# A two-layer streaming encoder in split fp32: sums of x, the last pair's factors and weight-sum transfers moved in the MLP

## The chip, the core and the metric

The kernel runs on one core of a Trainium2 chip. The metric is the device time of one execution in microseconds (us). The core has five engines that run side by side and meet only at semaphores: PE (TensorE, matrix products), DVE (VectorE), ACT (ScalarE), POOL (GpSimd) and SP (SyncE), of which SP and POOL here mostly start transfers. Each engine works off its own instructions in the order in which they were written out for it.

## The reference

Input is a prompt of 512 frames and a sample of 64 frames, model width 1024, so 576 columns of x in all. Layer 0 mixes tokens by pooling, layer 1 by sparse attention with a learned choice of keys. Each is followed by the same MLP, which takes most of the time and is what the change touches:

```python
def _mlp(h, w_up, w_down):          # w_up 1024 x 4096, w_down 4096 x 1024
    u = jax.nn.relu(h @ w_up)
    return (u * u) @ w_down

for i in range(DEPTH):              # 2 layers
    h = _rmsnorm(x, norm_mix[i])
    x = x + mixer(i, h)             # pooling mixer, or attention
    x = x + _mlp(_rmsnorm(x, norm_mlp[i]), mlp_w_up[i], mlp_w_down[i])
y = _rmsnorm(x, norm_final)
```

All of it is float32, and besides y the new pooling states and keys and values are returned.

## The kernel before

**Split products.** A float32 number is held as a high part (rounded by a cast) and a low part (the rest). A product of weights w and activations u is made of three matmuls: wh by uh, wh by ul, wl by uh. Each matmul has a 128x128 piece of weights and 288 columns, half of the 576 (HT).

**Units of weights.** Weights come in as raw blocks of 128x512 (256 KB) by transfers that SP starts. `split_unit` makes a unit of one: ACT casts the high part (wh, line 181), DVE subtracts it for the low part (wl, line 182). Six units can be held at a time. `made` yields units in the order in which they are used, and `next_unit(ahead=4)` draws from it until five are in hand and gives the first.

**Seven products for eight.** In the MLP the weight blocks are taken in pairs ("even" and "odd"), and two by two blocks of weights and of activations are multiplied with seven products in place of eight. This needs sums of weight blocks and seven factors of the activations (t3, t1, t2, b11, b22, b21, t4, numbered 0 to 6 in the tiles v and u). One sum of weights, s1, is loaded by a transfer of SP and one of POOL that adds to it in flight; a third transfer adds the even block to the odd one in place (`pair_sums`, lines 236 to 238); two further sums are made by DVE (lines 260 and 264). s1 and the second sum come from a pool of 3 buffers. `seven` makes one task of it: seven products of 12 matmuls each, in PSUM banks b, a and c; after a bank is complete a step of `Up` or `Down` reads it.

**A layer's MLP.** The hidden 4096 rows go in four chunks. Chunk 0's up projection is plain: eight blocks `up` (line 305), each pair giving one u (lines 455 to 483). While these run, DVE and ACT also make the factors of x that the later chunks need: `x_sums(j)` for j = 0 to 3 (tiles rough and xt, lines 431 to 435; one xt tile each; called after blocks 2, 3, 4 and 5), and `x_difference` after block 7 (tiles snap and xs, lines 440 to 443). Then chunk 0's down projection runs, four tasks `Down(q)`, each adding into x (line 536). Chunks 1 to 3 have four `Up(c, j)` tasks and then four `Down` tasks (three in the last chunk of layer 1). An `Up` task reads its banks (lines 565, 579, 585), squares on ACT (line 455), makes the seven factors in v (lines 476 to 483) and splits them into u by `parts_of`: a cast on ACT (line 472) and a subtraction on DVE (line 473). The tile v has one buffer, u has four, one for each pair of the chunk. The first product of a `Down` task is b11 over all four pairs, so it ends with the last pair's b11; the steps lo0, hi1, hi0 and lo1 of `Up` stand behind its last four products (b21, t3, b22, t4), in that order.

**What sets the order.** Nothing is ordered by hand on an engine. A scheduler takes the instructions in the order in which the code issues them, with waiting and buffers, and may let those of one engine pass each other; so a move in the code changes rows on every engine, which the section on the change shows.

## Time and profile before

| | |
|---|---|
| median of 3 runs | 1117.95 us (1115.55 to 1118.61) |
| profiled execution | 1120.28 us, its span 1118.5 us |
| mean granted clock of PE | 0.984 |
| PE busy | 1063.2 us, 95% of the span |
| DVE busy | 913.1 us, 82% |
| ACT busy | 626.0 us, 56% |
| POOL busy | 263.2 us, 24% |
| read from memory | 141.15 MB |

Times in the views are us from the start of the span. A row of the timeline gives start, length, engine, line, operation, output and inputs, and in brackets the idle time of the engine before it with the instruction that ended it. A matmul's length in such a row overlaps with the next one's, so the distance of two starts tells more than a length.

### The profile page before, as it was taken

The numbers are of one execution on the slowest core, as the hardware profiler recorded it, in microseconds if no ns is written. First come the engines' busy times: TensorE is split into PE (matmuls) and PEld (weight loads), VectorE is DVE, ScalarE is ACT, GpSimd is POOL, SyncE is SP. The second block draws the span as 40 slices with busy tenths as digits, with TensorE's granted clock in tenths as the row PEclk, the third lists the DMA queues.
The fourth block names the chain that finished last, engine by engine and source line by source line (L and its number), as shares of the span: only waits on it lengthen the run. The fifth ranks groups of instructions, "written<-read, shape, count | busy, mean of one in ns | idle before, by whom it ended". The sixth has DMA issues, their size and how long they took to land.

```text
span 1118.5 us, 21674 instructions
## 1 busy us (share of the span) xinstructions
PE 1063.2 (95%) x7942; PEld 1030.8 (92%) x7942; DVE 913.1 (82%) x1831; ACT 626.0 (56%) x1226; POOL 263.2 (24%) x285
## 2 busy tenths in 40 slices
PE   8998999999899899999989999999999999899896
PEld 8998999999899888999978888998998999899895
DVE  7788889879878967779997944689889879879974
ACT  8555456447546636354377776455457447547641
POOL 3100111111111100218696893000111111111101
PEclk9998999999999999999998999998999999999998
DMA  8222767576577564456641444433667566576512
GB/s 247 89 76 76 170 159 161 146 175 153 141 173 166 143 175 129 123 170 157 204 124 48 147 145 135 138 78 77 171 163 168 143 166 163 142 165 166 126 54 86
DMA packets 94459, 157.66 MB, mean 141 GB/s; under 512 B 13729, under 2 KB 25296, under 8 KB 94352
## 3 DMA queue, kind: packets, MB, share of 16 engines
q1 hardware_dynamic: 68720, 109.80, 32.3%
q0 software_dynamic: 15840, 28.84, 16.4%
q10 hardware_dynamic: 9792, 17.63, 5.2%
q8 instruction: 62, 1.02, 0.4%
q14 instruction: 45, 0.37, 0.1%
HBM read 141.15 MB, written 10.89 MB: 136 GB/s over the span
## 4 chain that ended last, share of the span: by engine, by line
PE 74%; DVE 12%; issue 5%; DMA 4%; ACT 2%; POOL 1%; SPq 1%; ACTq 0%; DVEq 0%; POOLq 0%
PE b L496 27%; PE c L496 14%; PE up L305 8%; PE a L496 7%; PE pj L305 3%; PE wo L305 3%; DVE wl L182 2%; PE wa L305 2%; PE sc L1219 2%; PE pt L1245 1%; PE pb L953 1%; DVE u L473 1%; PE o L1277 1%; PE dn L305 1%; PE o L1270 1%
## 5 line engine op out<-in xcount | busy, mean ns | idle before, releaser
L181 ACT CAST wh<-raw 128x512 fp32r<-128x512 f32 (+1 forms) x316 | 194.7, 620 | 247.6 <-PE b L496 86.5
L182 DVE TENSOR_TENSOR wl<-raw,wh 128x512 fp32r<-128x512 f32 (+1 forms) x294 | 205.7, 703 | 32.3 <-ACT wh L181 28.0
L496 PE MATMUL b<-u,wh 128*128 128x288 f32 x992 | 206.1, 299 | 21.1 <-DVE u L473 9.2
L496 PEld LDWEIGHTS b<-u,wh 128*128 128x128 f32 x992 | 160.3, 189 | 26.9 <-DVE u L473 11.0
L181 ACT CAST wh<-sum 128x512 fp32r<-128x512 f32 x165 | 101.8, 620 | 93.0 <-PE b L496 46.1
L496 PE MATMUL b<-u,wl 128*128 128x288 f32 x496 | 146.3, 297 | 0.0
L182 DVE TENSOR_TENSOR wl<-sum,wh 128x512 fp32r<-128x512 f32 x165 | 113.0, 688 | 32.8 <-ACT wh L181 27.6
L496 PE MATMUL c<-u,wh 128*128 128x288 f32 x496 | 105.4, 300 | 0.2
L238 POOL DMA_DIRECT2D raw<-in_w_down x31 | 26.7, 863 | 321.3 <-DMA raw<-in_w_down 111.8
L496 PEld LDWEIGHTS b<-u,wl 128*128 128x128 f32 x496 | 93.7, 190 | 0.3 <-DVE wl L182 0.2
L305 PE MATMUL up<-xs,wh 128*128 128x288 f32 x512 | 91.7, 302 | 1.0 <-DVE v L463 1.0
L473 DVE TENSOR_TENSOR u<-v,u 128x576 fp32r<-128x576 f32 (+3 forms) x86 | 80.0, 932 | 9.0 <-ACT u L472 8.4
L496 PE MATMUL b<-xt,wh 128*128 128x288 f32 x384 | 78.7, 298 | 8.4 <-DVE v L579 8.4
L496 PEld LDWEIGHTS c<-u,wh 128*128 128x128 f32 x496 | 81.4, 191 | 2.1 <-DVE x L536 1.5
L305 PEld LDWEIGHTS up<-xs,wh 128*128 128x128 f32 x512 | 77.3, 194 | 1.9 <-DVE v L463 1.5
L472 ACT CAST u<-v 128x576 fp32r<-128x576 f32 (+3 forms) x86 | 69.6, 815 | 14.5 <-DVE v L480 8.4
L496 PE MATMUL b<-xs,wh 128*128 128x288 f32 x384 | 77.5, 295 | 0.0
L496 PE MATMUL c<-u,wl 128*128 128x288 f32 x248 | 74.1, 299 | 0.0
L496 PEld LDWEIGHTS b<-xt,wh 128*128 128x128 f32 x384 | 61.1, 188 | 11.2 <-DVE v L579 11.2
L305 PE MATMUL pj<-xs,wh 128*128 128x288 f32 x352 | 61.9, 295 | 1.3 <-ACT xs L294 1.3
L455 ACT ACTIVATE v<-v 128x288 f32<-128x288 f32 (+1 forms) x112 | 51.8, 475 | 17.1 <-DVE v L565 10.0
L496 PEld LDWEIGHTS b<-xs,wh 128*128 128x128 f32 x384 | 61.4, 188 | 0.0
(281 smaller groups left out, 2692.1 us busy)
## 6 DMA issues: line engine op xcount, KB each, us to landing
raw<-in_w_up SPq DMA_DIRECT2D x128, 256.0 KB, 3.0
raw<-in_w_down SPq DMA_DIRECT2D x128, 256.0 KB, 3.1
raw<-in_w_o ACTq DMA_DIRECT2D x32, 256.0 KB, 3.2
sum<-in_w_down SPq DMA_DIRECT2D x31, 256.0 KB, 3.1
sum<-in_w_down POOLq DMA_DIRECT2D x31, 256.0 KB, 4.7
raw<-in_w_down POOLq DMA_DIRECT2D x31, 256.0 KB, 4.5
raw<-in_w_in ACTq DMA_DIRECT2D x30, 256.0 KB, 3.2
sum<-in_w_up SPq DMA_DIRECT2D x24, 256.0 KB, 2.9
```

The lines of the kernel that those rows point to most:

```text
L181: act.copy(h, src)
L182: how["sub"].tensor_tensor(l, src, f32(h), ALU.subtract)
L238: pool.dma_start(raw, even[:, :512], accum_op=ALU.add)
L305: pe.matmul(pt[h][:, :m] if isinstance(pt, tuple) else pt[:, h, :m], wt, xs[k][:, part, c:c + m], start=(k == 0 and i == 0), stop=(k == n ...
L455: act.activation(v, v, AF.Square)
L472: act.copy(u[:, f, 0], v[:, f])
L473: dve.tensor_tensor(u[:, f, 1], v[:, f], f32(u[:, f, 0]), ALU.subtract)
L496: pe.matmul(bank[:, :HT], wt, ut, start=first and j == 0 and i == 0, stop=j == 3 and i == 2, skip_group_check=True)
L953: pe.matmul(pt[:, c0:c0 + rhs.shape[1]], lhs, rhs, start=n == 0, stop=n == len(steps) - 1)
L1219: pe.matmul(pt[:, hh, :nw], q[:, 2 * s + hh], ks[g][:, part, :nw], start=part == 0, stop=part == 1)
L1245: pe.transpose(pp[:, c:c + P], pr[:, hh, kt * P:(kt + 1) * P], ident)
L1270: pe.matmul(oc[:, 2 * s + hh], pT[:, c:c + P], V[:, kt, vs], start=kt == 0, stop=kt == i)
```

## The change

Four edits, all in the MLP; the computation stays the same.

1. The transfers for s1 go out with the pair's first block instead of with the odd block (`sum_of`); only the addition of the even block to the odd one stays there. The pool of sums has 4 buffers instead of 3.
2. In `seven`, units are drawn one at a time at fixed places (`ahead`, after each bank's step, up to LEAD = 5 in hand) instead of by `next_unit`.
3. In `Up`, the last pair of a chunk splits its factor 3 (b11) by itself right behind lo0 and factor 4 in hi0. In the other pairs factors 3 and 4 are split in hi0 instead of hi1. Factors 0 to 2 are split in lo1 instead of hi0.
4. `x_sums` 0 and 1 are issued after plain blocks 3 and 5, and 2 and 3 after the loop over the blocks, ahead of `x_difference`.

```diff
--- before.py
+++ after.py
@@ -49,6 +49,7 @@
 MLP_BLOCKS = ("up", "even", "odd", "down")
 PLAIN_CHUNKS = 1
 SEEDED = 4
+LEAD = 5
 UP_ORDER = (0, 4, 1, 5, 2, 6, 3, 7)
 FACTORS = ("t3", "t1", "t2", "b11", "b22", "b21", "t4")
 
@@ -211,10 +212,11 @@
                 raw.append(raw_tile(pool_, size)[:, :n // 2])
                 self.live[at].append(raw[-1])
                 (nc.sync if mlp else act).dma_start(raw[-1], src[:, i * n // 2:(i + 1) * n // 2])
+                if kind == "even" and i == 0:
+                    self.even, self.sum = src, sum_of(jobs[1][1])
                 if kind == "odd" and i == 0:
-                    self.blocks[-1][3].append(pair_sums(raw[0], self.even, src))
-                if kind == "even":
-                    self.even = src
+                    pool.dma_start(raw[0], self.even[:, :512], accum_op=ALU.add)
+                    self.blocks[-1][3].append(self.sum)
                 if i:
                     jobs.pop(0)
 
@@ -230,12 +232,11 @@
             self.fill()
             return self.blocks.pop(0) if self.blocks else None
 
-    def pair_sums(raw, even, odd):
+    def sum_of(odd):
 
         s1 = phase["sums"].tile([P, 512], F32, tag="sum", name=uid("sum"))
         nc.sync.dma_start(s1, odd[:, :512])
         pool.dma_start(s1, odd[:, 512:], accum_op=ALU.add)
-        pool.dma_start(raw, even[:, :512], accum_op=ALU.add)
         return s1
 
     def made():
@@ -498,32 +499,50 @@
 
         tasks = [0]
 
+        def ahead(n=1):
+
+            how["sub"] = dve
+            for _ in range(n):
+                if len(ready) < LEAD:
+                    u = next(units, None)
+                    if u is not None:
+                        ready.append(u)
+
+        def take():
+            if not ready:
+                ahead()
+            return ready.pop(0)
+
         def seven(operand, late, on):
 
 
             b, a_, c = (psum1(t) for t in "bac")
             on.banks = [t[:, :HT] for t in (a_, b, c)]
-            w = next_unit()
+            w = take()
             product(b, w, operand, "b11", rows, True)
             tasks[0] += 1
             if tasks[0] <= SEEDED:
                 pe.matmul(a_[:, :HT], w[0][:, :P], operand(0, "b11", 0), start=True, stop=True, skip_group_check=True)
             act.copy(a_[:, :HT], b[:, :HT])
-            w1 = next_unit()
+            ahead()
+            w1 = take()
             if late:
-                w2 = next_unit()
+                w2 = take()
                 product(c, w1, operand, "t1", rows[:3], True)
                 product(b, w2, operand, "t2", rows[:3])
                 product(c, w1, operand, "t1", rows[3:])
                 on.c()
+                ahead()
                 product(b, w2, operand, "t2", rows[3:])
             else:
                 product(c, w1, operand, "t1", rows, True)
                 on.c()
-                product(b, next_unit(), operand, "t2", rows)
+                ahead()
+                product(b, take(), operand, "t2", rows)
             on.b()
+            ahead()
             for bank, factor, then in ((a_, "b21", on.lo0), (b, "t3", on.hi1), (c, "b22", on.hi0), (b, "t4", on.lo1)):
-                product(bank, next_unit(), operand, factor, rows)
+                product(bank, take(), operand, factor, rows)
                 then()
 
         class Down:
@@ -543,21 +562,25 @@
 
             def lo0(self):
                 self.update(self.lo[0], 0, ALU.add)
+                ahead()
 
             def hi1(self):
                 self.update(self.hi[1], 1, ALU.subtract)
+                ahead()
 
             def hi0(self):
                 self.update(self.hi[0], 2, ALU.add)
+                ahead()
 
             def lo1(self):
                 self.update(self.lo[1], 1, ALU.subtract)
+                ahead()
 
         class Up:
 
 
             def __init__(self, c, j):
-                self.at = c, j
+                self.at, self.final = (c, j), j == half - 1
                 self.v, self.u = tiles()
 
             def relu(self, i, src, op, h):
@@ -573,12 +596,15 @@
 
             def lo0(self):
                 self.relu(3, self.banks[0], ALU.max, 1)
+                ahead()
+                if self.final:
+                    parts_of(self.u, self.v, slice(3, 4))
 
             def hi1(self):
                 v = self.v
                 dve.tensor_tensor(v[:, 4], self.banks[1], snap[:, 0], ALU.add)
                 self.relu(4, v[:, 4], ALU.min, 0)
-                parts_of(self.u, v, slice(3, 5))
+                ahead()
 
             def hi0(self):
                 v = self.v
@@ -586,15 +612,22 @@
                 self.relu(0, v[:, 0], ALU.max, 0)
                 if end and self.at[0] == 3:
                     left_over(self.at[1], v[:, 0])
+                parts_of(self.u, v, slice(4 if self.final else 3, 5))
                 first_sum(v)
                 middle_sums(v)
-                parts_of(self.u, v, slice(0, 3))
 
             def lo1(self):
                 v = self.v
                 self.relu(5, self.banks[1], ALU.min, 1)
+                if not self.final:
+                    ahead()
+                parts_of(self.u, v, slice(0, 3))
                 last_sum(v)
+                if not self.final:
+                    ahead()
                 parts_of(self.u, v, slice(5, 7))
+                if self.final:
+                    ahead(2)
 
         def spread():
 
@@ -646,8 +679,11 @@
                     for t in todo:
                         finished(*t)
                     todo.clear()
-                    if c == 0 and 2 <= i < 6:
-                        x_sums(i - 2)
+                    if c == 0 and 3 <= i < 7 and i % 2:
+                        x_sums(i // 2 - 1)
+                if c == 0:
+                    x_sums(2)
+                    x_sums(3)
                 if c == PLAIN_CHUNKS - 1:
                     snap = halves(tmp("snap", "s2", 1))
                     for j in range(half):
@@ -1415,13 +1451,13 @@
     with stage(more=RAWS[1]):
         with stage(xs=1, slots=1, tmps=6, ps=3, po=2):
             pool_mixer()
-        with stage(xs=1, u=1, acts=1, xt=1, sums=3, ps=2, po=4):
+        with stage(xs=1, u=1, acts=1, xt=1, sums=4, ps=2, po=4):
             mlp(0, 1, late=KT)
     with stage(under=1, xs=1, slots=1, cst2=1, tmps=5), ExitStack() as parts:
         const([P, UNDER], "pad", pool=phase["under"])
         parts.enter_context(stage(ps=2, po=4))
         attention(parts)
-    with stage(u=1, xs=1, acts=1, xt=1, sums=3, more=RAWS[1], ps=2, po=4):
+    with stage(u=1, xs=1, acts=1, xt=1, sums=4, more=RAWS[1], ps=2, po=4):
         mlp(1, 3, end=last)
```

On the engines this gives DVE and ACT six instructions more each, and the same number of transfers. Three places in the order:

The passage from an up phase to its down phase, on DVE. Here v_2317 is the last pair of chunk 1 in layer 0, u_2318 its split factors, wl_ a weight split, snap_ the copies of banks. Before:

```order
297 L565 SCALAR_TENSOR_TENSOR v_2317<-a_2320,rbm_148_863 128x288
298 L579 TENSOR_TENSOR v_2317<-b_2319,snap_1283 128x288
299 L585 TENSOR_TENSOR v_2317<-c_2321,snap_1283 128x288
300 L565 SCALAR_TENSOR_TENSOR v_2317<-v_2317,rbm_148_863 128x288 x2
301 L476 TENSOR_TENSOR v_2317<-v_2317 128x288
302 L565 SCALAR_TENSOR_TENSOR v_2317<-b_2319,rbm_148_863 128x288
303 L479 SCALAR_TENSOR_TENSOR v_2317<-v_2317 128x288
304 L473 TENSOR_TENSOR u_2318<-v_2317,u_2318 128x2x288
305 L480 TENSOR_TENSOR v_2317<-v_2317 128x288
306 L182 TENSOR_TENSOR wl_2495<-sum_2381,wh_2494 128x512
307 L483 SCALAR_TENSOR_TENSOR v_2317<-v_2317 128x288
308 L260 TENSOR_TENSOR sum_2534<-sum_2364,raw_2298 128x512
```

After (v_2320 and u_2321 are the same pair):

```order
298 L265 TENSOR_TENSOR sum_2395<-sum_2395,raw_2187 128x512
299 L588 SCALAR_TENSOR_TENSOR v_2320<-a_2323,rbm_149_866 128x288
300 L611 TENSOR_TENSOR v_2320<-c_2324,snap_1286 128x288
301 L605 TENSOR_TENSOR v_2320<-b_2322,snap_1286 128x288
302 L183 TENSOR_TENSOR wl_2494<-raw_2223,wh_2493 128x512
303 L588 SCALAR_TENSOR_TENSOR v_2320<-v_2320,rbm_149_866 128x288 x2
304 L474 TENSOR_TENSOR u_2321<-v_2320,u_2321 128x288
305 L477 TENSOR_TENSOR v_2320<-v_2320 128x288
306 L588 SCALAR_TENSOR_TENSOR v_2320<-b_2322,rbm_149_866 128x288
307 L480 SCALAR_TENSOR_TENSOR v_2320<-v_2320 128x288
308 L481 TENSOR_TENSOR v_2320<-v_2320 128x288
309 L183 TENSOR_TENSOR wl_2522<-sum_2395,wh_2521 128x512
```

The read of bank c (now line 611) passed that of bank b (now line 605), the first subtraction for u takes one part instead of two and stands three rows behind the read of b, and a pair sum and a weight split stand elsewhere.

The start of layer 0's first down product, on DVE. u_901 is the second pair of chunk 0, u_1054 the third, xt_ the sums of x. Before:

```order
129 L435 TENSOR_TENSOR xt_1057<-rough_686,xt_1057 128x3x288
130 L413 TENSOR_SCALAR negative_9160<-gv 128x8
131 L182 TENSOR_TENSOR wl_1153<-sum_924,wh_1152 128x512
132 L435 TENSOR_TENSOR xt_1137<-rough_686,xt_1137 128x3x288
133 L473 TENSOR_TENSOR u_901<-v_900,u_901 128x7x288
134 L463 SCALAR_TENSOR_TENSOR v_1053<-up_1004,rbm_148_863 128x2x288
135 L463 SCALAR_TENSOR_TENSOR v_1053<-up_1080,rbm_148_863 128x576
136 L476 TENSOR_TENSOR v_1053<-v_1053 128x288
137 L479 SCALAR_TENSOR_TENSOR v_1053<-v_1053 128x288
138 L480 TENSOR_TENSOR v_1053<-v_1053 128x288
139 L483 SCALAR_TENSOR_TENSOR v_1053<-v_1053 128x288
140 L473 TENSOR_TENSOR u_1054<-v_1053,u_1054 128x7x288
```

After, u_904 is the second pair and u_1050 the third; first the rows around the second pair, then those up to the third:

```order
113 L183 TENSOR_TENSOR wl_1054<-raw_746,wh_1053 128x512
114 L477 TENSOR_TENSOR v_903<-v_903 128x288
115 L480 SCALAR_TENSOR_TENSOR v_903<-v_903 128x288
116 L481 TENSOR_TENSOR v_903<-v_903 128x288
117 L484 SCALAR_TENSOR_TENSOR v_903<-v_903 128x288
118 L183 TENSOR_TENSOR wl_1060<-raw_821,wh_1059 128x512
119 L474 TENSOR_TENSOR u_904<-v_903,u_904 128x7x288
120 L432 SCALAR_TENSOR_TENSOR rough_686<-x_81,gv,rough_686 128x288 x2
```

```order
138 L436 TENSOR_TENSOR xt_1123<-rough_686,xt_1123 128x3x288
139 L265 TENSOR_TENSOR sum_1130<-sum_1130,raw_912 128x512
140 L484 SCALAR_TENSOR_TENSOR v_1049<-v_1049 128x288
141 L183 TENSOR_TENSOR wl_1205<-raw_912,wh_1204 128x512
142 L444 TENSOR_TENSOR xs_642<-snap_1286,xs_642 128x288
143 L414 TENSOR_SCALAR negative_9166<-gv 128x8
144 L436 TENSOR_TENSOR xt_1272<-rough_686,xt_1272 128x3x288
145 L436 TENSOR_TENSOR xt_1279<-rough_686,xt_1279 128x3x288
146 L183 TENSOR_TENSOR wl_1321<-raw_918,wh_1320 128x512
147 L441 TENSOR_TENSOR snap_1286<-xs_657,xs_645 128x576
148 L474 TENSOR_TENSOR u_1050<-v_1049,u_1050 128x7x288
```

The second pair's subtraction (now line 474) stands ahead of every rough and xt row; the four xt rows, with pair sums, weight splits and the first rows of xs and snap, stand between it and the third pair's.

The end of layer 0, on POOL, whose rows here are the transfers that add in flight. sum_4990 is s1 of the last pair of weights in this layer. Before:

```order
75 L237 DMA sum_4840<-in_w_down 128x512
76 L1178 MEMSET mask_6014 128x128
77 L1185 MEMSET inverse 128x2
78 L1179 MEMSET mask_6014 64x64
79 L238 DMA raw_4838<-in_w_down 128x512
80 L237 DMA sum_4990<-in_w_down 128x512
81 L238 DMA raw_4988<-in_w_down 128x512
```

After, the same sum is sum_4951:

```order
74 L239 DMA sum_4814<-in_w_down 128x512
75 L218 DMA raw_4718<-in_w_down 128x512
76 L239 DMA sum_4951<-in_w_down 128x512
77 L218 DMA raw_4873<-in_w_down 128x512
78 L1214 MEMSET mask_6020 128x128
```

The sum's transfer went from behind the masks and a raw block to ahead of both; each sum stands one raw block earlier.

## The prediction

> **What bounds the kernel now.** I read the engine summary first, then the windows by stage, the waits, and at the waits the timeline. TensorE (PE) is the bound:
>
> ```profile
> PE 1063.2 (95%) x7942; PEld 1030.8 (92%) x7942; DVE 913.1 (82%) x1831; ACT 626.0 (56%) x1226; POOL 263.2 (24%) x285
> 149.60:193.60 44.00, 43.23 (x326) 42.76 (x324) 40.83 (x77) 29.55 (x59) 6.91 (x8) 1.00 0.67 166
> 205.70:249.00 43.30, 43.30 (x330) 43.30 (x329) 33.06 (x58) 18.95 (x34) 6.77 (x8) 1.00 0.74 177
> ```
>
> The last two rows are windows (length; busy PE, weight load, DVE, ACT, POOL; granted clock; DMA share; GB/s). The first is an up phase, the second a down phase. In the down phase PE has no gap and DVE is idle for 10 us of 43; in the up phase DVE is busy for 40.83 of 44.00, so it ends the phase with a backlog. PE's own matmuls are not touched by this change, so it can win only where PE waits. The waits that name this code:
>
> ```profile
> PEld b L496 <- DVE v L579: 11.2, 12, 1.6
> PE b L496 <- DVE u L473: 9.2, 8, 2.0
> PE b L496 <- ACT u L472: 6.4, 8, 1.8
> PE b L496 <- DVE x L536: 4.0, 2, 2.6
> ```
>
> (What waits, for whom; total us, times, longest.) They lie in three kinds of place.
>
> First, each of the six passages from an up phase to its down phase. One of them on PE, and DVE at the same time:
>
> ```profile
> 192.80 0.29 PE L496 MATMUL b<-u,wl 128*128 128x288 f32 x1
> 194.45 0.53 PE L496 MATMUL b<-xt,wh 128*128 128x288 f32 x2 [1.36 <-DVE v L579]
> 196.01 0.29 PE L496 MATMUL b<-xt,wl 128*128 128x288 f32 x1
> 196.59 0.40 PE L496 MATMUL b<-u,wh 128*128 128x288 f32 x1 [0.29 <-ACT u L472]
> 197.92 0.40 PE L496 MATMUL b<-u,wh 128*128 128x288 f32 x1 [0.93 <-DVE u L473]
> 199.48 0.29 PE L496 MATMUL c<-u,wh 128*128 128x288 f32 x1
> 200.05 0.53 PE L496 MATMUL b<-u,wh 128*128 128x288 f32 x2 [0.28 <-ACT a L511]
> 192.37 1.29 DVE L182 TENSOR_TENSOR wl<-raw,wh 128x512 fp32r<-128x512 f32 x2
> 193.95 0.45 DVE L579 TENSOR_TENSOR v<-b,snap 128x288 f32<-128x288 f32 x1
> 194.31 0.45 DVE L585 TENSOR_TENSOR v<-c,snap 128x288 f32<-128x288 f32 x1
> 194.68 0.82 DVE L565 SCALAR_TENSOR_TENSOR v<-v,rbm 128x288 f32<-128x288 f32 x2
> 196.00 0.46 DVE L476 TENSOR_TENSOR v<-v 128x288 f32<-128x288 f32 x1 [0.51 <-ACT v L455]
> 196.38 0.45 DVE L565 SCALAR_TENSOR_TENSOR v<-b,rbm 128x288 f32<-128x288 f32 x1
> 196.74 0.45 DVE L479 SCALAR_TENSOR_TENSOR v<-v 128x288 f32<-128x288 f32 x1
> 197.11 0.75 DVE L473 TENSOR_TENSOR u<-v,u 128x576 fp32r<-128x576 f32 x1
> ```
>
> Running matmuls start 0.133 us apart (two in 0.42 less overlap; 12 in 1.59). Against that the starts show losses of 194.45-192.80-0.13 = 1.52, then 0.45, 1.20 and 0.44: 3.6 us a passage. The last passage, next to the kernel's end, has three of the same waits and loses about as much:
>
> ```profile
> 1049.79 0.53 PE L496 MATMUL b<-xt,wh 128*128 128x288 f32 x2 [0.40 <-DVE v L579]
> 1053.14 0.40 PE L496 MATMUL b<-u,wh 128*128 128x288 f32 x1 [1.48 <-ACT u L472]
> 1054.60 0.40 PE L496 MATMUL b<-u,wh 128*128 128x288 f32 x1 [1.06 <-DVE u L473]
> ```
>
> Second, the start of the first down product of each layer, where DVE works off x_sums, the four splits of sums of x:
>
> ```profile
> 80.25 1.04 DVE L435 TENSOR_TENSOR xt<-rough,xt 128x864 fp32r<-128x864 f32 x1
> 81.22 0.51 DVE L433 SCALAR_TENSOR_TENSOR rough<-x,negative,rough 128x288 f32<-128x288 f32 x1
> 81.65 1.04 DVE L435 TENSOR_TENSOR xt<-rough,xt 128x864 fp32r<-128x864 f32 x1
> 86.20 2.24 DVE L473 TENSOR_TENSOR u<-v,u 128x2016 fp32r<-128x2016 f32 x1
> 85.83 0.40 PE L496 MATMUL b<-u,wh 128*128 128x288 f32 x1 [1.71 <-ACT u L472]
> 88.50 0.61 PE L496 MATMUL b<-u,wh 128*128 128x288 f32 x1 [2.00 <-DVE u L473]
> 82.50:89.00 6.50, 2.73 (x14) 1.88 (x13) 6.47 (x9) 3.21 (x3) 1.04 (x2) 0.82 0.53 121
> 89.00:93.30 4.30, 4.30 (x20) 4.30 (x19) 2.55 (x6) 2.65 (x3) 0.43 (x1) 0.50 0.41 66
> 93.30:105.00 11.70, 11.70 (x90) 11.70 (x90) 10.45 (x17) 5.73 (x12) 0.00 (x0) 0.99 0.12 46
> 93.84 2.26 DVE L473 TENSOR_TENSOR u<-v,u 128x2016 fp32r<-128x2016 f32 x1 [2.00 <-ACT u L472]
> 105.87 0.53 PE L496 MATMUL b<-u,wh 128*128 128x288 f32 x2
> 112.42 0.40 PE L496 MATMUL a<-u,wh 128*128 128x288 f32 x1 [0.44 <-DVE u L473]
> ```
>
> About 3.8 us are waits there (1.71+2.00), and the clock falls to 0.50 for 4.3 us, worth another 4.3/2 = 2.1 us.
>
> Third, the end of layer 0, where one pair sum waits for a transfer and holds DVE's queue, with PE behind it:
>
> ```profile
> 399.68 0.86 POOL L237 DMA_DIRECT2D sum<-in_w_down  x1 [7.11 <-DVE x L536]
> 405.99 0.69 DVE L260 TENSOR_TENSOR sum<-sum,raw 128x512 f32<-128x512 f32 x1 [4.01 <-DMA sum<-in_w_down]
> 409.63 0.54 PE L496 MATMUL b<-u,wh 128*128 128x288 f32 x2 [2.60 <-DVE x L536]
> ```
>
> **The change part by part.** *Last pair split by itself.* It adds six ACT casts and six DVE subtractions (one a passage), some 0.37 us each by the start-to-start of the 0.45 us rows above. They stand in front of the product that PE waits for, so they are counted in the walk below. In the old order DVE needs, from the start of L579 (193.95) to the end of the two-part subtraction (197.11+0.75), 3.91 us. In the new order the same read (now L605) is followed by one weight split (0.60: the two at 192.37 take 1.29 in all, one 0.69), two L588 (0.74) and the one-part subtraction: 0.37+0.60+0.74+0.45 = 2.16 us, 1.75 less. The t4 product between takes 1.59, so of the 0.45+1.20 that PE loses before and in that product about 0.15 is left: 1.5 us gained. The cast for it needs only v's part 3, made before L605, so ACT's 0.51 drops out of this path.
>
> The first wait (1.52) can move either way: L605 stands behind L611 now (+0.37), but one pair sum is done earlier, in the idle of a down phase (-0.60), and the nine matmuls that stand next to t4 in front of the wait are ordered otherwise: they come before t3, so that less is left to fill it. I take -0.2, bounds +0.4 and -0.8. Behind it, the rest of u (one, three and two parts) is done about 6.8 us after the start of L605 in the new order, 7.7 before; I take 0.3 from that, with 0 and 0.6 as bounds. Sum a passage 1.5+0.2+0.3 = 2.0 (0.8 to 2.9); six of them **-12.0** (-5 to -17). The last passage has further splits of left-overs among these rows and I take it like the others.
>
> *Splitting units at fixed places.* The same casts and subtractions (0.60 each on DVE) go out one after each bank instead of by a count of units in hand. In an up phase PE and DVE both have nearly no room; PE ran without a gap there before, and the order of the products changes by half a product at most. I cost it at nothing; its cover is the weight unit made ahead, about one product (1.59 us). Bounds: 0 and +1 a passage.
>
> *Two sums of x.* In the code two of four x_sums move behind the plain up blocks. On DVE all four still stand ahead of the third pair's subtraction; what changes is that the second pair's comes first. So the waits at 85.83 and 88.50 go, and PE runs on: the 96 up matmuls begin near 83.8 and end at 83.8+96*0.133 = 96.6. But DVE then has, between the two subtractions, 12 rough rows (0.43), four xt subtractions (0.97), five weight splits and two pair sums (0.60), two 576-wide v (0.67), four 288-wide (0.37), and snap and xs pieces (1.2): 5.2+3.9+4.2+1.3+1.5+1.2 = 17.3, from about 80.4 (the second pair's subtraction ended at 88.44 behind 9.1 us of these sums; without them 79.3, and I add 1.1 for ACT's casts on the way). With the 2.2 of the subtraction it is ready at 99.9, 3.3 after PE ran dry; the fourth pair's first factors come 5.8 later (two v of 576, three of 288, snap, xs, a weight split, two one-part subtractions, an ACT square), and the next product (b, 105.87 before) starts near 106.9: +1.0. PE was nearly idle for 9 us, so its clock will be halved as at 89.00 before: +2.1. What it lost at 112.42 (0.44 and a second such gap, 0.8 together) goes: -0.8. Sum +2.3 a layer, two layers **+4.6**. Bounds for each: -4 (DVE's rows come sooner, no cold clock) and +5.
>
> By the Trainium skill ("TensorE: Matmul & The Clock Gate", HAM oscillation), an idle stretch of some 3.4 us halves the clock, and sustained work of that length releases it; the trace halves it after waits of 1.71 and 2.00 with a few matmuls between, so here shorter gaps did it. By the rule the new 3.3 us wait alone would be on the edge, and without a cold clock the two layers would come to +0.4 instead of +4.6 (1103.6 in all, near the third rival's 1103).
>
> *Transfers.* Per pair the 256 KB load of the sum (SP) and its accumulate (POOL) go out at the first block, ahead of the odd block's loads; number and bytes stay. Moved past are SP's two raw loads and POOL's accumulate into raw. At the end of layer 0 POOL's issue was at 399.68 and the data came at 405.99; in the new order it stands in front of the previous raw accumulate and hangs on an earlier weight split, several units of 1.59 us earlier. DVE's 4.01 wait needs 4.0, so it goes, and with it PE's 2.60: **-2.8** with the restart (0 to -4). Elsewhere no DVE wait for these transfers shows in the list above, and the DMA engines were 0.67 and 0.74 busy, so nothing more is gained. Late next would be the raw block behind a sum that waits for its buffer; the fourth sums buffer works against that.
>
> Sum: -12.0 + 4.6 - 2.8 = -10.2. The profiled execution took 1120.28 us (span 1118.5), 2.3 above the median of 1117.95. So 1110.1 for an execution like that one, and 1107.8 against the median: **1108**.
>
> **The rivals.**
> *DVE only shifts its backlog* (same). The up phases leave DVE 3 us of 44; if what is saved by splitting the factor alone is spent on the sums and splits now placed in front of it, a passage gains 0.4 and the starts still cost: -2.4+4.6-2.8 = -0.6, about 1117.5. For it: 40.83 of 44.00. Against: the rows that stand between are counted above.
> *The layer starts decide* (slower). The x_sums now stand between second and third pair. If each start costs +5 (a cold clock through 9 us of dribbled matmuls and DVE's backlog carried into the first down tasks), and the passages give only 0.8: +10-4.8 = +5, 1123. It wins when the starts lose more together than the passages give. For it: 17.3 us of DVE in one piece with a dry PE. Against: the DVE row counts end at 99.9, not later.
> *The starts win as well* (faster still). If the third pair's split is done when the up blocks end, the cold clock goes: -4 each, with -2.0 a passage and -2.8: -22.8, 1095; with the starts at zero 1103. For it: DVE was idle for 2.00 us before 93.84 in the old order. Against: its order still has all four sums in front.
> *The sums are not moved into the down projection at all*: that is how I read the order, and it is part of the forecast, not a case beside it.
>
> **How the numbers follow.** Forecast (-10, within 1103 to 1114) 0.53; starts win (1095 to 1103) 0.20; backlog shifts (1114.6 to 1121) 0.14; starts decide (over 1121) 0.13. A change of 0.3% (3.4 us) is about what this kernel's runs can tell. Leaving out the best half of the second case and the worst of the last gives 1099 to 1120. Faster 0.75, same 0.13, slower 0.12.
>
> **What the new profile would show.** PE's wait for L473's successor (L474) inside the passages near 0.2 and the wait for L605 near 1.3; no wait at the first down product for the second pair, but a wait of 3 us after the up blocks for the third, with a clock near 0.5 behind it; no 4 us DVE wait for a sum near 400. I'd be wrong if new waits for weight splits (wl) appear in PE's list, if the wait for L605 grows past 2 us, or if the third pair is ready when the up blocks end.

## The result, and the profile after

The changed kernel takes 1105.66 us (median, 1104.97 to 1110.1), the kernel before 1117.51 on the same occasion: 11.85 us less, a ratio of 0.9904 with the 95% interval [0.9875, 0.9934]. The forecast was 1108 in 1099 to 1120. One execution of the control further down took 1171.98 us at a granted clock of 0.844; no median or ratio here counts it. The profiled execution took 1105.90 us with this summary:

```profile
span 1104.1 us, 21662 instructions
PE 1058.5 (96%) x7942; PEld 1030.0 (93%) x7942; DVE 910.8 (82%) x1837; ACT 628.7 (57%) x1232; POOL 263.4 (24%) x285
```

The span is 14.4 us shorter, and DVE and ACT issue six instructions more each. PE's 1058.5 is 4.7 less for the same 7942 matmuls, but a second profile of the kernel before (the control below) has 1059.1, so most of that difference belongs to the execution and not to the change. The waits that name this code, as before (what waits, for whom; total us, times, longest):

```profile
PE b L497 <- DVE v L605: 6.8, 6, 1.1
PE b L497 <- DVE u L474: 6.7, 4, 2.9
PE b L497 <- ACT u L473: 5.1, 2, 2.5
PE b L497 <- ACT a L526: 2.2, 3, 1.0
PE b L497 <- DVE x L555: 1.4, 1, 1.4
```

PE now waits for the factors' subtraction (L474) 4 times instead of 8, and all four are at the layer starts. In the passages the wait for the read of bank b (L605) is left, 6 times 1.1; the last passage of layer 1 also has a new one of 0.98 for ACT's copy of a bank (L526). The first passage on PE and DVE:

```profile
196.43 0.53 PE L497 MATMUL b<-xt,wh 128*128 128x288 f32 x2 [1.14 <-DVE v L605]
198.00 0.29 PE L497 MATMUL b<-xt,wl 128*128 128x288 f32 x1
198.13 0.43 PE L497 MATMUL b<-u,wh 128*128 128x288 f32 x2
195.56 0.45 DVE L611 TENSOR_TENSOR v<-c,snap 128x288 f32<-128x288 f32 x1
195.92 0.46 DVE L605 TENSOR_TENSOR v<-b,snap 128x288 f32<-128x288 f32 x1
196.29 0.69 DVE L183 TENSOR_TENSOR wl<-raw,wh 128x512 fp32r<-128x512 f32 x1
196.88 0.83 DVE L588 SCALAR_TENSOR_TENSOR v<-v,rbm 128x288 f32<-128x288 f32 x2
197.62 0.46 DVE L474 TENSOR_TENSOR u<-v,u 128x288 fp32r<-128x288 f32 x1
```

From the start of L605 to the end of the one-part subtraction are 197.62+0.46-195.92 = 2.16 us, and t4's last matmul (198.00) is followed by the last pair's b11 after 0.13, so PE doesn't stop. The start of layer 0's first down product, timeline and then windows (length; busy PE, weight load, DVE, ACT, POOL; granted clock; DMA share; GB/s):

```profile
97.61 2.27 DVE L474 TENSOR_TENSOR u<-v,u 128x2016 fp32r<-128x2016 f32 x1
99.93 0.40 PE L497 MATMUL b<-u,wh 128*128 128x288 f32 x1 [2.88 <-DVE u L474]
103.27 0.61 PE L497 MATMUL b<-u,wh 128*128 128x288 f32 x1 [2.54 <-ACT u L473]
106.69 0.85 PE L497 MATMUL b<-u,wh 128*128 128x288 f32 x2 [0.62 <-ACT a L526]
82.50:97.00 14.50, 14.50 (x111) 14.32 (x109) 14.50 (x29) 9.75 (x13) 0.00 (x0) 1.00 0.21 54
97.00:107.00 10.00, 3.43 (x12) 2.43 (x12) 10.00 (x19) 4.66 (x10) 0.86 (x1) 0.72 0.34 79
107.00:112.00 5.00, 5.00 (x23) 5.00 (x23) 5.00 (x11) 2.04 (x4) 0.85 (x1) 0.53 0.37 111
```

PE runs through to 97, then waits for the third pair (ready at 99.88) and the fourth, with DVE busy all the time, and runs on at a clock of 0.53 for 5 us. The end of layer 0, where the sum's accumulate now goes out 13.6 us earlier (some 4 of them because the layer up to here is shorter) and no wait for its transfer is left:

```profile
386.07 0.86 POOL L239 DMA_DIRECT2D sum<-in_w_down  x1 [11.51 <-DVE u L474]
400.00:409.00 9.00, 9.00 (x70) 9.00 (x69) 6.57 (x12) 3.46 (x7) 0.86 (x1) 1.00 0.79 224
```

By stage, from the starts of the first matmul with the same weight unit in both profiles (us, minus is faster):

| stage | forecast | profile before to after |
|---|---|---|
| start of layer 0's down projection | +2.3 | +2.9 |
| passages of layer 0 | 3 x -2.0 | -2.3, -2.3, -2.4 |
| end of layer 0 | -2.8 | -4.3 |
| attention | 0 | -2.4 |
| start of layer 1's down projection | +2.3 | +3.0 |
| passages of layer 1 | 3 x -2.0 | -2.4, -2.3, -2.2 |

This compares one execution with one execution; the control at the end of the experiments shows which of these differences appear without the change.

### The profile page after: what moved, and what is told of

It reads as the page before. It is cut to its first block, busy times and chain, and to the rows that moved or that the text cites. A ratio compares the mean times of both kernels' runs of the same rounds, so it can differ in the third digit from the quotient of the medians.

```text
span 1104.1 us, 21662 instructions
## 1 busy us (share of the span) xinstructions
PE 1058.5 (96%) x7942; PEld 1030.0 (93%) x7942; DVE 910.8 (82%) x1837; ACT 628.7 (57%) x1232; POOL 263.4 (24%) x285
## 4 chain that ended last, share of the span: by engine, by line
PE 80%; DVE 9%; ACT 4%; POOL 2%; issue 2%; DMA 1%; SPq 0%; DVEq 0%; ACTq 0%; POOLq 0%
PE b L497 28%; PE c L497 14%; PE up L306 8%; PE pj L306 7%; PE a L497 7%; PE wo L306 3%; DVE wl L183 2%; PE sc L1255 2%; PE wa L306 1%; PE v L1155 1%; PE pt L1281 1%; PE pb L989 1%; PE dn L306 1%; DVE u L474 1%; ACT wh L182 1%
## 5 line engine op out<-in xcount | busy, mean ns | idle before, releaser
L239 POOL DMA_DIRECT2D sum<-in_w_down x31 | 27.1, 891 | 338.0 <-DVE u L474 125.2
L306 PE MATMUL up<-xs,wh 128*128 128x288 f32 x512 | 89.2, 296 | 1.0 <-DVE v L464 1.0
L474 DVE TENSOR_TENSOR u<-v,u 128x576 fp32r<-128x576 f32 (+3 forms) x92 | 81.0, 888 | 6.2 <-ACT u L473 6.2
L306 PEld LDWEIGHTS up<-xs,wh 128*128 128x128 f32 x512 | 74.7, 188 | 1.9 <-DVE v L464 1.4
L239 POOL DMA_DIRECT2D sum<-in_w_up x24 | 20.7, 863 | 214.6 <-DVE wl L183 147.8
```

The costliest lines, as they stand in the source:

```text
L239: pool.dma_start(s1, odd[:, 512:], accum_op=ALU.add)
L306: pe.matmul(pt[h][:, :m] if isinstance(pt, tuple) else pt[:, h, :m], wt, xs[k][:, part, c:c + m], start=(k == 0 and i == 0), stop=(k == n ...
L474: dve.tensor_tensor(u[:, f, 1], v[:, f], f32(u[:, f, 0]), ALU.subtract)
```

## The experiments

Each time is a median with its ratio to runs of the kernel before on the same chip in the same stretch (before: 1116.87, 1116.59 and 1117.32 us in the three stretches). The first four runs take one part of the change back, or carry one further.

**The last pair's factor not split by itself.** The four `parts_of` calls of `Up` stand where they were, everything else as changed.

```diff
-                if self.final:
-                    parts_of(self.u, self.v, slice(3, 4))      # lo0
+                parts_of(self.u, v, slice(3, 5))               # hi1
-                parts_of(self.u, v, slice(4 if self.final else 3, 5))
+                parts_of(self.u, v, slice(0, 3))               # hi0, behind the sums
-                parts_of(self.u, v, slice(0, 3))               # lo1
```

(Shortened; the comments name the steps.)

> The changed kernel with the splits of factors put back where they were: 3 and 4 together in hi1, 0 to 2 in hi0, for the last pair too. Theory (the last pair's b11 split alone is what shortens each passage from up to down): in DVE's order the subtraction that PE waits for now comes behind the read of bank b, a weight split, two L588, four more 288-wide rows and another weight split, 0.37+0.60+0.74+1.48+0.60+0.75 = 4.5 us after the read instead of 2.2, so each of the six passages loses 2.0 to 2.5 and the kernel takes 1118 to 1121 us. Rival (the passages gained because pair sums and unit splits moved, not by the factor): within 3 us of the changed kernel, 1103 to 1109.

1124.96 us, 1.0072 [1.0050, 1.0094]: slower than before the change, and 4 us above the theory's upper end. The profiled execution, the shortest of its runs (1120.42), shows the passage of the theory:

```profile
195.48 0.44 DVE L603 TENSOR_TENSOR v<-b,snap 128x288 f32<-128x288 f32 x1
195.98 0.53 PE L497 MATMUL b<-xt,wh 128*128 128x288 f32 x2 [1.14 <-DVE v L603]
199.01 0.40 PE L497 MATMUL b<-u,wh 128*128 128x288 f32 x1 [1.15 <-ACT u L473]
200.42 0.40 PE L497 MATMUL b<-u,wh 128*128 128x288 f32 x1 [1.01 <-DVE u L474]
199.61 0.75 DVE L474 TENSOR_TENSOR u<-v,u 128x576 fp32r<-128x576 f32 x1
196.00:206.00 10.00, 7.84 (x55) 7.37 (x56) 9.46 (x18) 6.23 (x12) 0.86 (x1) 1.00 0.43 122
294.00:299.00 5.00, 5.00 (x27) 5.00 (x27) 3.46 (x6) 2.15 (x5) 0.86 (x1) 0.66 0.49 123
```

From the start of the read of bank b (L603) to the end of the two-part subtraction are 199.61+0.75-195.48 = 4.88 us, where the theory had 4.5 and the changed kernel has 2.16. The theory missed what the last two rows show: behind the same three waits the clock stayed at 1.00 in the first passage and fell to 0.66 in the second. From the first of the three waits to that of the next passage are 93.43 us for the first passage and 94.82 for the second, 1.4 more. Two more of the six passages of this execution lost clock, one of them the last, which does so in the kernel before too. The three that kept it could add some 4.2 us in other runs; that would fit the median and not the longest run (1128.57), and no profile here shows either.

**x_sums at their old places.**

```diff
-                    if c == 0 and 3 <= i < 7 and i % 2:
-                        x_sums(i // 2 - 1)
-                if c == 0:
-                    x_sums(2)
-                    x_sums(3)
+                    if c == 0 and 2 <= i < 6:
+                        x_sums(i - 2)
```

> The changed kernel with x_sums called after plain blocks 2, 3, 4 and 5 again. Theory (the move costs 2.9 us at the start of each layer's first down product, since all four sums now stand between the second and the third pair): waits near 86 and 88 come back in place of those near 100 and 103, and the kernel takes 5 to 6 us less, 1099 to 1102. Rival (the move is neutral, what is lost at the start comes from the units' new places): 1104 to 1107.

1103.93 us, 0.9886 [0.9867, 0.9904]: less than the changed kernel, between the ranges of theory and rival. Its profile has the old waits back, and layer 0's start is at the old time again to 0.03 us:

```profile
86.24 0.40 PE L497 MATMUL b<-u,wh 128*128 128x288 f32 x1 [1.72 <-ACT u L473]
88.90 0.61 PE L497 MATMUL b<-u,wh 128*128 128x288 f32 x1 [2.00 <-DVE u L474]
```

Since the changed kernel had been timed elsewhere, both ran again side by side.

> The changed kernel once more, beside the next run on one chip. Theory (the move of x_sums costs 2.9 us at each layer's start, as the first run of the next kernel's profile shows): 4 to 6 us more than the next run. Rival (part of that price comes back elsewhere, since the two medians lay only 1.7 us apart): 1 to 3 us more.

> x_sums at their old places, all else as in the changed kernel, beside the run above: theory 4 to 6 us less than it, rival 1 to 3 us less.

1105.73 (0.9894 [0.9879, 0.9908]) against 1100.93 (0.9859 [0.9843, 0.9875]): 4.8 us, inside the theory's range and outside the rival's. The move of the sums costs about 5 us. Between the two profiles of the kernel with the sums at their old places, the attention alone, which the edit does not touch, differs by 3.2 us: from the last wait of layer 0's MLP to the first up product of layer 1 are 279.55 us in the first and 276.34 in the second.

**Transfers at the odd block again, 3 sums buffers.**

```diff
-                if kind == "even" and i == 0:
-                    self.even, self.sum = src, sum_of(jobs[1][1])
+                    self.even = src                             # "even"
+                    self.sum = sum_of(src)                      # "odd"
-        with stage(xs=1, u=1, acts=1, xt=1, sums=4, ps=2, po=4):
+        with stage(xs=1, u=1, acts=1, xt=1, sums=3, ps=2, po=4):
```

> The changed kernel with s1's transfers issued with the odd block again and 3 sums buffers. Theory (the early transfers only remove DVE's wait for the last sum of layer 0 and PE's stall with its half clock): 3 to 5 us more, 1109 to 1111, with a DVE wait of some 4 us near 400 back; the passages keep their gain. Rival (early sums also let DVE do pair sums ahead in the down phases, which is what shortens the passages): 1113 to 1118, with longer waits in the passages.

1114.40 us, 0.9974 [0.9961, 0.9987]: 8.7 more than the changed kernel's 1105.66. The theory's 1109 to 1111 is missed and the time lies in the rival's range, though the profile says that each had a part:

```profile
197.04 0.54 PE L498 MATMUL b<-xt,wh 128*128 128x288 f32 x2 [1.32 <-DVE v L606]
203.73 0.40 PE L498 MATMUL c<-u,wh 128*128 128x288 f32 x1 [0.38 <-DVE u L475]
407.40 0.53 PE L498 MATMUL b<-u,wh 128*128 128x288 f32 x2 [2.10 <-DVE x L556]
```

The stall at the end of layer 0 is back, and each passage gains 1.5 us against before instead of 2.3, so the passages keep most of their gain, against the rival.

**Three sums buffers, transfers still early.** The only edit is `sums=3`.

> The changed kernel with 3 sums buffers instead of 4, transfers still issued with the first block. DVE's order at the passage is that of the run with the transfers undone (the pair sum and a weight split stand behind the factor again). Theory (it is the fourth buffer, not the time of issue, that lets DVE do pair sums ahead): each passage gains 1.5 instead of 2.3 and the time is that of the run with the transfers undone, 1111 to 1116. Rival (the time of issue does it): 1104 to 1108.

1115.65 us, 0.9983 [0.9973, 0.9994], within the theory's range: with three buffers the earlier issue gains nothing. DVE waits 3.7 us for a sum's transfer at the end of layer 0 again, PE 2.23 behind it, and the passages gain the 1.5 of the run before. Whether the fourth buffer alone would do, with the transfers at the old place, wasn't run.

Then three parts by themselves on the kernel before. The new places of the other pairs' splits, the second half of the third edit, were not run by themselves.

**Only the units' places** (`take` and `ahead` in `seven`, `Up` and `Down`).

> The kernel before with the units drawn one at a time at fixed places, and nothing else of the change. Theory (the places alone do nothing): DVE's order at the passage is that of before, row by row, so the same four waits per passage, the same stall at the end of layer 0: 1114 to 1119 us, no difference from before. Rival (drawing units evenly is itself a gain, DVE's backlog shrinks): at least 4 us less than before, and the wait for bank b's read under 1.2.

1116.85 us, 1.0005 [0.9996, 1.0014]: nothing, as forecast.

**Only the last pair's factor.**

```diff
                 self.relu(3, self.banks[0], ALU.max, 1)
+                if self.final:
+                    parts_of(self.u, self.v, slice(3, 4))
...
-                parts_of(self.u, v, slice(3, 5))
+                parts_of(self.u, v, slice(4 if self.final else 3, 5))
```

> The kernel before with the last pair's factor 3 split by itself behind lo0 and factor 4 in hi1, nothing else. In DVE's order the one-part subtraction comes 0.37+0.37+0.74+0.45 = 1.9 us after the start of bank b's read instead of 3.9. Theory: each passage loses its second and third wait, 1.2 to 1.7 us, and the other terms stay: 7 to 10 us less than before, 1107 to 1110. Rival (the factor needs the other edits to pay): less than 4 us gained.

1108.15 us, 0.9927 [0.9911, 0.9942], in the theory's range. The passage keeps the wait for bank b's read, loses the next two, and has 0.40 in their place:

```profile
193.93 0.53 PE L496 MATMUL b<-xt,wh 128*128 128x288 f32 x2 [1.36 <-DVE v L581]
200.61 0.40 PE L496 MATMUL c<-u,wh 128*128 128x288 f32 x1 [0.40 <-DVE u L473]
193.43 0.44 DVE L581 TENSOR_TENSOR v<-b,snap 128x288 f32<-128x288 f32 x1
194.90 0.45 DVE L473 TENSOR_TENSOR u<-v,u 128x288 fp32r<-128x288 f32 x1
```

**Only the transfers** (issued with the first block, 4 buffers).

> The kernel before with s1's transfers issued with the pair's first block and 4 sums buffers, nothing else. In DVE's order the read of bank c passes that of bank b, and a weight split and four more 288-wide rows come ahead of the subtraction that PE waits for, as in the first run (split undone). Theory (the transfers save 4.3 at the end of layer 0 by themselves but lengthen the passages where the factor isn't split alone): 1112 to 1119, little or no gain against before, with waits of about 1.1, 1.2 and 1.0 in each passage. Rival (the early transfers are worth 4.3 there and 0.75 a passage whatever else is done): 1107 to 1110.

1115.80 us, 0.9996 [0.9986, 1.0005]: no gain, as the theory has it. Its passages are those of the run with the split undone:

```profile
194.01 0.53 PE L496 MATMUL b<-xt,wh 128*128 128x288 f32 x2 [1.10 <-DVE v L579]
197.00 0.40 PE L496 MATMUL b<-u,wh 128*128 128x288 f32 x1 [1.15 <-ACT u L472]
198.40 0.40 PE L496 MATMUL b<-u,wh 128*128 128x288 f32 x1 [1.00 <-DVE u L473]
```

Alone the parts come to 0, -8.4 and -0.8; together, without the move of x_sums, to -12.9 and -16.4 in its two runs. So at least the factor and the transfers need each other: the early sums put a weight split and more rows in front of what PE waits for, and no wait is left of them once the waited-for part is split alone. What the other pairs' splits add to this is not shown.

Two runs carry the idea of the title further.

**Two sums of x really in the down projection.** x_sums(2) and (3) are issued after the first task of chunk 0's down projection. In the changed kernel their scratch, rough, shares its four buffers with u, and the fourth pair's u is the fifth tile there; so here it is taken from v.

```diff
+            if j == 2:
+                late_rough.append(phase["acts"].tile([P, 7, HT], F32, tag="v", bufs=1, name=uid("v")))
...
-                if c == 0:
-                    x_sums(2)
-                    x_sums(3)
...
                 seven(of(us), q == 0, Down(q))
+                if c == 0 and q == 0:
+                    x_sums(2)
+                    x_sums(3)
```

> The changed kernel with x_sums(2) and x_sums(3) issued after the first task of chunk 0's down projection, their scratch taken from the one buffer of v, so that the fourth pair's u (which takes the buffer of rough) need not wait for them. Theory (two sums between the second and third pair's subtraction cost the start): without them the third pair's subtraction is ready near 94, before the up blocks end at 96.6, the long gap and the half clock go, and each layer's start is 6 to 8 us shorter than in the changed kernel: 1090 to 1095. Rival (the start is bound by the chain of the fourth pair behind the up blocks, ACT included, whatever stands ahead): a wait of 3 us or more and the half clock stay, 1101 to 1106.

1095.73 us, 0.9811 [0.9793, 0.9829], 0.7 above the theory's range and far below the rival's:

```profile
92.55 2.26 DVE L480 TENSOR_TENSOR u<-v,u 128x2016 fp32r<-128x2016 f32 x1 [0.62 <-ACT u L479]
98.18 0.40 PE L503 MATMUL b<-u,wh 128*128 128x288 f32 x1 [0.17 <-ACT u L479]
99.54 0.40 PE L503 MATMUL b<-u,wh 128*128 128x288 f32 x1 [0.96 <-DVE u L480]
102.00:107.00 5.00, 4.95 (x28) 4.71 (x28) 4.10 (x8) 2.03 (x5) 1.25 (x2) 0.74 0.48 108
```

The third pair is ready at 94.81 instead of 99.88, the long gap is gone, and the clock still falls to 0.74 for a while after the short ones. The move without the new scratch was not run, so how much each of the two gives is not shown.

**And the other two sums earlier**, ahead of the first pair's factors:

```diff
-                    if c == 0 and 3 <= i < 7 and i % 2:
-                        x_sums(i // 2 - 1)
+                    if c == 0 and i == 2:
+                        x_sums(0)
+                        x_sums(1)
                     for t in todo:
                         finished(*t)
```

> The run with two sums in the down projection, with x_sums(0) and x_sums(1) issued ahead of the first pair's factors instead of after blocks 3 and 5. DVE's order puts their rows among the sums of squares of the norm. Theory A (DVE has room there: it is busy for only 6.5 of 10 us and 5.2 of 10 us between 50 and 70): the third and fourth pair come earlier, the waits near 98 to 101 go, 2 to 5 us less than that run in the two layers, 1090 to 1094. Theory B (the norm's chain is on the path there, 4.5 us of rows ahead of it make PE wait near 63): the same or up to 8 us more, 1096 to 1104.

1091.98 us, 0.9784 [0.9771, 0.9797], the fastest of all, as theory A has it; theory B's wait is there, but small:

```profile
65.31 0.80 PE L306 MATMUL up<-xs,wh 128*128 128x288 f32 x4 [1.28 <-DVE v L470]
101.07 0.53 PE L503 MATMUL b<-u,wh 128*128 128x288 f32 x2 [0.48 <-ACT a L532]
102.00:107.00 5.00, 5.00 (x39) 5.00 (x39) 4.97 (x10) 2.03 (x4) 1.71 (x2) 1.00 0.58 121
```

PE waits 1.28 near 65 instead of 0.50, and at the start of the down projection 0.48 is left, at full clock.

**The kernel before once more**, as a control.

> The kernel before, profiled once more, as a control for stages that the change doesn't touch. Theory (differences of one or two us in the attention and at the end of layer 0 between two profiles belong to the execution, not to the program): the attention and the stall at the end of layer 0 differ by 1 to 3 us from the first profile, the passages and layer starts by less than 0.5. Rival: every stage agrees within 0.3.

1116.62 us, 0.9992 [0.9982, 1.0003]. Layer 0's start and passages agree with the first profile within 0.1 us; the start of layer 1 is 0.5 us shorter. The end of layer 0 does not:

```profile
404.53 0.69 DVE L260 TENSOR_TENSOR sum<-sum,raw 128x512 f32<-128x512 f32 x1 [2.40 <-DMA sum<-in_w_down]
408.18 0.53 PE L496 MATMUL b<-u,wh 128*128 128x288 f32 x2 [0.98 <-DVE x L536]
408.00:413.00 5.00, 4.82 (x36) 4.83 (x37) 3.44 (x7) 2.06 (x4) 0.00 (x0) 1.00 0.40 135
```

DVE waits 2.40 instead of 4.01, PE 0.98 instead of 2.60, and the clock stays at 1.00; this part is 3.1 us shorter in the same program, and the attention 2.4.

## Why the prediction was right, step by step

*The passages* were the largest term, -2.0 each, and measured -2.2 to -2.4. The 2.16 us that the rows of the old trace gave for the new order are 2.16 in the new trace. The second and third wait went whole, where 0.15 was kept, and the first went from 1.52 to 196.43-195.00-0.13 = 1.30, as taken. For the rest of u 0.3 was taken, and the fourth loss went from 0.44 to 0.28 only. Another 0.3 comes from a wait in the middle of the up phase, some 12 us ahead of the passage, which no step of the forecast lists:

```profile
182.12 0.54 PE L496 MATMUL b<-xt,wh 128*128 128x288 f32 x2 [0.26 <-DVE v L579]
```

By the starts it costs 0.42 us, and 0.11 in the new profile. It stands in five of the six up phases of the kernel before. In that of the passage shown it is there in every profile with the old transfers or three buffers, and gone in every one with the new transfers and four buffers. Without the factor split the passage is as long as before or longer, with it alone it gains 1.6.

That the last passage of layer 1 came out like the others (-2.2) is luck. By the starts its waits cost 3.6 us before and 3.2 after, since a wait for ACT's copy and two short ones take the place of the two that went. The rest is clock, which fell behind the old waits and not behind the new ones, and which the forecast did not count there. The first row is before, the others are after:

```profile
1055.00:1060.00 5.00, 5.00 (x28) 5.00 (x28) 3.98 (x8) 2.63 (x5) 0.00 (x0) 0.66 0.18 56
1042.37 0.53 PE L497 MATMUL b<-u,wh 128*128 128x288 f32 x2 [0.98 <-ACT a L526]
1047.00:1052.00 5.00, 5.00 (x39) 5.00 (x39) 5.00 (x11) 2.70 (x6) 0.33 (x1) 1.00 0.48 105
```

*The layer starts* were forecast at +2.3 and cost +2.9 and +3.0 (2.8 and 3.4 against the control's profile); the two runs side by side give 4.8 for both. The count of DVE's rows up to the third pair's subtraction gave 99.9; it ended at 99.88, and the steps of the count hold too (the second pair's subtraction ended at 80.54 where 80.4 was taken). Two sizes were too small. The next product on bank b starts at 106.69; counted from the first up product of each profile (41.12 and 41.51) it is 1.2 later than before, not 1.0. And 2.1 us were taken for the clock from the old stretch of 4.3 us at 0.50, where the new one is 5 us at 0.53 (2.35) behind 10 us at 0.72. The forecast had also weighed the rule of the Trainium skill ("TensorE: Matmul & The Clock Gate", HAM oscillation) that the clock falls behind idle gaps of more than some 3.4 us. The rule fails here behind the change as well: the clock fell, and PE's longest single gap there is 2.88.

*The end of layer 0* is the term that was mis-sized: -2.8 forecast, -4.3 between the two profiles. The step that failed took only the wait of 2.60 and its restart, and missed the clock behind it in the trace of before:

```profile
409.00:414.00 5.00, 4.37 (x22) 4.38 (x23) 2.83 (x6) 1.53 (x3) 0.00 (x0) 0.69 0.27 98
```

That is 5 x 0.31 = 1.55 us more. But the control shows that the term isn't constant: against that profile it is worth 4.3-3.1 = 1.2. In the runs of the places alone and of the factor alone, whose transfers are those of before, PE waits 0.94 and 2.15 there, and the clock stays at 1.00 in both.

*The attention's* -2.4 was in no step, and belongs to the execution: the control has it without the change, and over all profiles here the stretch from the last wait of layer 0's MLP to the first up product of layer 1 takes 274.2 to 279.6 us. The first profile of before lay above the median by more than the profile after does, which is why the spans differ by 14.4 and the medians by 11.85.

*Units' places at nothing* holds by itself. *The transfers* were costed with the end of layer 0 alone; the runs show that the early sums with the fourth buffer also give 0.8 of the 2.3 in each passage. The walk of the order had counted the part of it that shortens the first wait, without saying whose it was; the wait in the middle of the up phase it had not.

*The rivals.* DVE's backlog did not eat the gain of the factor. The starts cost less than the passages gave. That the sums weren't moved into the down projection was right: when they were, the time fell by another 10 us, to 1095.73, about the third rival's 1095.

*Sums that do not follow from their terms.* The rival in which the layer starts decide leaves out the transfers' -2.8; with it, it would come to about 1120 and not 1123. The lower bound of a passage, 0.8, is 1.1 by its own terms (1.5-0.4). In the rows of before the rest of u ends 8.1 us behind the start of the read of bank b, not 7.7, and in those of after 7.2, not 6.8; only the difference, 0.9, was right. None of these moves the forecast.

## What to carry to other kernels

When an engine waits for one part of a group that another engine finishes together, split that part alone and count, in the new order, the rows between the last event and the waited-for part; with durations from the old trace this count was right to 0.1 us here, while what hung on the granted clock or a transfer was off by 0.6 to 1.5, and one passage came out right mainly through the clock. A right sum does not show this; the waits of each place have to be compared one by one. A move in the code is a move on the engine only where the buffers allow it: with three sums buffers the earlier issue was worth nothing. So read the order, and where a scratch tile shares its buffers with what is waited for, try another one for it; the run here that did this changed both at once. Parts of a change should be run alone and taken away: here the last pair's factor gave most by itself, the units' places nothing, the transfers nothing unless the factor was there, and the move of the sums, which was only taken back, cost 5 us.

## What the runs showed of the hardware that was not expected

The granted clock falls behind waits of one to three us, and not every time. With the split undone, the same three waits of 1.14, 1.15 and 1.01 us within 5 us left it at 1.00 in one passage and 0.66 in another of the same execution. Behind a single wait of 2.10 and one of 2.23 at the end of layer 0 it was 1.00 and 0.66:

```profile
408.00:413.00 5.00, 5.00 (x40) 5.00 (x39) 3.17 (x6) 2.52 (x5) 0.00 (x0) 1.00 0.53 174
408.00:413.00 5.00, 5.00 (x28) 5.00 (x28) 2.17 (x5) 2.07 (x4) 0.00 (x0) 0.66 0.46 172
```

(Windows of the run with the transfers undone and of the run with three sums buffers: 40 and 28 matmuls in the same 5 us.) These two alone would also fit a limit between 2.10 and 2.23; the passages fit no limit on the length of the waits. What decides there is not shown.

In the last passage of layer 1 the outcome goes with the kernel. The five without the factor split have a clock of 0.66 over 5 us there, in the kernel before behind waits that cost 1.65 and 1.33 us by the starts; the nine with the split have 1.00.

By the starts such a fall costs 1.4 to 1.5 us on top of the wait: 94.82 against 93.43 between the passages above, and in the two profiles of the kernel before 23.81 against 22.29 from the wait at the end of layer 0 to the next one. Whether it also makes runs spread is open: the two kernels with three such waits in each passage range from 1120.42 to 1128.57 (split undone) and from 1114.71 to 1117.99 (transfers alone).
